# Low-rank parameter tiles in the places of the attention values, not in the residual stream's pool

## The chip, the cores and the metric

One NeuronCore of a Trainium2 chip runs the kernel. The metric is the device time of one execution in microseconds (us). The engines are named as in the profile: PE (TensorE, matmuls), PEld (its weight loads), DVE (VectorE), ACT (ScalarE), POOL (GpSimd) and SP (SyncE, which here only issues transfers).

## The reference

One layer of a streaming encoder, 512 tokens of width 1024, all in float32: a half-step SwiGLU, a mixer of two branches, a second half-step SwiGLU, and a final RMSNorm.

```python
x = x + 0.5 * swiglu(rms_norm(x, ffn1_norm[l]), ffn1_w1[l], ffn1_w3[l], ffn1_w2[l])
h = rms_norm(x, mix_norm[l])
p = h @ w_in[l]
p_rwkv = token_shift(p[..., :SHIFT_COLS], shift_mu[l])
p_fox = p[..., SHIFT_COLS:SHIFT_COLS + FOX_COLS]
gates = jax.nn.sigmoid(p[..., SHIFT_COLS + FOX_COLS:])
...
y_a = rwkv7_mixer(p_rwkv, ...) @ rwkv_proj[l]
y_b = fox_mixer(p_fox, f_bias, q_norm, k_norm) @ fox_proj[l]
x = x + (gate_a * y_a + gate_b * y_b) @ w_out[l]
x = x + 0.5 * swiglu(rms_norm(x, ffn2_norm[l]), ffn2_w1[l], ffn2_w3[l], ffn2_w2[l])
return rms_norm(x, final_norm)
```

What the change touches is the start of `rwkv7_mixer`. The decay and the in-context rate of its recurrence come from low-rank codes of the input projection, each through a small matrix of 32 rows:

```python
w_log = -jax.nn.softplus(-(w0 + jnp.tanh(w_lo) @ w_up)) - 0.5
a = jax.nn.sigmoid(a0 + a_lo @ a_up)
```

## The kernel before

Features lie on the 128 partitions and the 512 tokens along a row, so the residual stream is eight tiles `xT0` to `xT7` of 128 x 512. For accuracy each operand of a large matmul is split into a rounded part and the rest (`xh` and `xl`, `whi` and `wlo`), and a product is three matmuls (`mm3`, L130 to L132). A column of 128 outputs from 1024 inputs is therefore 24 matmuls. Its weights come as one transfer of 512 KB from SP's queue into `raw` (three buffers); ACT rounds them to `whi` (L122) and DVE takes the difference to `wlo` (L123), two buffers each. Columns of the projection go into a PSUM pool of two banks (`pm`), in turn.

The mixer begins at about 373 us with the low-rank codes (`pl`). Then come, for each of the four head pairs p, the columns k, r, v (`column`, PSUM `pk`) and a gate column (`plain_gate`, PSUM `pgt`), in the function `step(p)`. `column` empties the bank on DVE into a tile `u` (three buffers), multiplied by the norm's `rstd`, and `shifted` mixes `u` with its copy one token earlier, half on ACT, half on DVE. The key then gets its gain and its square (`ksq`, split into `khi` and `klo`), the sum of squares by a matmul `pn`, its inverse root (`krn`); the products go into `G` and `BK`, and `gp` are small matmuls between these.

Between the codes and the columns stand eight matmuls `pz` (L493): for each p one of `uw` (the matrix of the decay) and one of `ux` (that of the rate) with the codes. ACT turns each into a sigmoid (L494), DVE scans the decays along each chunk of 32 tokens with `cmask` (L565).

`uw` and `ux` are made early, on POOL, from `loraw`, which a transfer fills; `rows` holds the small parameters until one transpose puts them into `par`. The gains of the first norm come through a tile `g1` of their own.

Memory at the right edge is a stack of pools. The pool `xr1` holds the residual tiles `xT` and, before the change, also `g1`, `rows`, `loraw`, `uw` and `ux`. After the last `pz` is written down in the program, `xctx.close()` ends it (L496). Then `vtp` is opened, with four places `vt0` to `vt3` of 128 x 512 for the attention values (filled much later, at the columns `pv`) and a small pad, and above it `t2`, which holds `cmask`, `u`, the `k`/`r` tiles and the work tiles of `step`. A tile of a pool that takes over ended pools' memory waits until the ended pool's readers and writers are through. The residual itself has been saved by eight transfers `xsave` from POOL's queue (L408) and is read back later.

The order on each engine is set by a scheduler that simulates the program while it is built, from these waits, the order of the code and a few pins (`issue_after`, `keep_in_program_order`). A wait that vanishes can therefore change the order too.

Of the kernel before, what the change touches and what calls it, by code (L numbers as in the profile page):

```python
# [9 lines left out]
F32 = mybir.dt.float32  # L10
F32R = mybir.dt.float32r
# [7 lines left out]
P = 128  # L19
T = 512  # L20
# [4 lines left out]
DA = 512  # L25
# [3 lines left out]
NB = T // P  # L29
# [8 lines left out]
PAR_N = 69  # L38
# [13 lines left out]
def kernel(  # L52
# [6 lines left out]
    nc = tc.nc  # L59
    dve, act, pool, pe = nc.vector, nc.scalar, nc.gpsimd, nc.tensor  # L60
# [10 lines left out]
    def bank(name, pool_=None):  # L71
        pool_ = pool_ or pm
        return pool_.tile([P, T], F32, tag="b", name=name)
# [5 lines left out]
    ident = cp.tile([P, P], F32, name="ident")  # L79
# [76 lines left out]
        return cast  # L156


    xctx = ExitStack()
    rtp = xctx.enter_context(tc.tile_pool(name="xr1", bufs=1, side="right"))  # L160
    xT = [rtp.tile([P, T], F32, name=f"xT{c}") for c in range(KD)]
# [67 lines left out]
        return par[:, i:i + 1]  # L229


    g1 = rtp.tile([8, P], F32, name="g1")
    nc.scalar.dma_start(g1[:], ffn1_norm[0].rearrange("(a b) -> a b", b=P))
    warm = bank("warm", pf)
    for _ in range(8):
        pe.matmul(warm[:, 0:P], ones_[:], ones_[:], start=True, stop=True)
    gtp = bank("gtp", pr)
    pe.transpose(gtp[:, 0:8], g1[:], ident[0:8, 0:8])
    dve.tensor_copy(par[:, 0:8], gtp[:, 0:8])
    nrm = Norm(PAR_FFN1)  # L240
    with tc.tile_pool(name="x0", bufs=1) as x0:
# [26 lines left out]

    pin = pool.memset(onec[:], 1.0)
    tc.keep_in_program_order(pin)  # L270
    rows = rtp.tile([PAR_N, P], F32, name="rows")
    loraw = rtp.tile([P, DA], F32, name="loraw")
    uw, ux = [rtp.tile([96, DA], F32R, name=n) for n in ("uw", "ux")]
    q0, q1, q2 = slice(0, 32), slice(32, 64), slice(64, 96)

    def f32(ap):
        return ap.bitcast(F32)

    pool.memset(rows[:], 0.0)

    def masks():
        pool.memset(gmask[:], 1.0)
# [34 lines left out]

    def place_params():
        ptp = bank("ptp")
        pe.transpose(ptp[:, 0:PAR_N], rows[:], ident[0:PAR_N, 0:PAR_N])  # L320
        dve.tensor_copy(par[:, 8:PAR_N], ptp[:, 8:PAR_N])
        dve.tensor_scalar(par[:, PAR_Q:PAR_Q + 1], par[:, PAR_Q:PAR_Q + 1], 0.125, None, op0=ALU.mult)
        pool.tensor_copy(uw[q0], loraw[q0, :])
        pool.tensor_copy(uw[q1], loraw[q0, :])
        pool.tensor_tensor(uw[q2], loraw[q0, :], f32(uw[q0]), op=ALU.subtract)
        pool.tensor_copy(ux[q0], loraw[q1, :])
        pool.tensor_copy(ux[q2], loraw[q1, :])
        pool.tensor_copy(ux[q1], loraw[q1, :])
        pool.tensor_tensor(ux[q1], loraw[q1, :], f32(ux[q1]), op=ALU.subtract)
# [89 lines left out]
    with ExitStack() as mx:  # L419
# [74 lines left out]
                tc.keep_in_program_order(act.activation(o, ps[:], AF.Sigmoid, bias=pc(par0 + p)))  # L494
        logs = tc.keep_in_program_order(act.preload_act_table_set("natural_log_exp_and_others"))
        xctx.close()  # L496
        fctx = ExitStack()
        vtp = fctx.enter_context(tc.tile_pool(name="vtp", bufs=1, side="right"))
        vts = [vtp.tile([P, T], F32, name=f"vt{b}", tag=f"vt{b}") for b in range(NB)]
        vtp.tile([P, 48], F32, name="vtpad", tag="vtpad")  # L500
        pctx = ExitStack()
        t2 = pctx.enter_context(tc.tile_pool(name="t2", bufs=1, side="right"))
        cmask = t2.tile([P, T], F32, name="cmask")
# [148 lines left out]
        for t in range(C - 1):  # L652
            n, m = t + 1, C - 1 - t
# [67 lines left out]
        vt = []  # L721
# [109 lines left out]
        for p in range(NP):  # L831
# [16 lines left out]
            for i, bl in enumerate(((0, 1), (2,), (3,))):  # L848
# [3 lines left out]
                for q in range(2):  # L852
                    lp = pf.tile([P, T], F32, tag="b", name="lp")
                    lps.append(lp)
                    for b in bl:
                        n, bs = (b + 1) * P, slice(b * P, (b + 1) * P)
# [4 lines left out]
                for q in range(2):  # L861
                    pt, mx = pts[:, q], mx_[q]
                    for b in bl:
                        n, mb = (b + 1) * P, mx[:, b:b + 1]
# [107 lines left out]
        rtp = ctx.enter_context(tc.tile_pool(name="xr2", bufs=1, side="right"))  # L972
# [94 lines left out]
```

## Time and profile before

| | us |
|---|---|
| median of 3 runs | 1195.16 |
| lowest and highest | 1194.19, 1195.84 |
| the profiled execution's own time | 1195.16 |
| its span, first to last instruction | 1193.5 |

The mean granted clock of TensorE over the span is 0.994 of full speed. In the timeline a row begins with start and duration in us from the span's start; then come engine, line, operation, output and inputs, shapes, and in brackets how long the engine had been idle before it and what released it. Rows of waits give the total, the number of times and the longest. Rows of stretches give each engine's busy time with the number of instructions, then the granted clock, the share of the DMA engines and GB/s. Matmuls overlap, so their pace is read from start to start.

### The profile page before, as it was taken

The numbers are of one execution on the slowest core, as the hardware profiler recorded it, in microseconds if no ns is written. First come the engines' busy times: TensorE is split into PE (matmuls) and PEld (weight loads), VectorE is DVE, ScalarE is ACT, GpSimd is POOL, SyncE is SP. The second block draws the span as 40 slices with busy tenths as digits, with TensorE's granted clock in tenths as the row PEclk, the third lists the DMA queues.
The fourth block names the chain that finished last, engine by engine and source line by source line (L and its number), as shares of the span: only waits on it lengthen the run. The fifth ranks groups of instructions, "written<-read, shape, count | busy, mean of one in ns | idle before, by whom it ended". The sixth has DMA issues, their size and how long they took to land.

```text
span 1193.5 us, 15868 instructions
## 1 busy us (share of the span) xinstructions
PE 1172.4 (98%) x6334; PEld 953.9 (80%) x6334; DVE 663.8 (56%) x993; ACT 458.3 (38%) x739; POOL 101.1 (8%) x144
## 2 busy tenths in 40 slices
PE   8999999999999999999999999999999999999997
PEld 7888888888887788887767777778888888888887
DVE  6545444533444698676756657866554545443242
ACT  6322222222224755346876656523222222222221
POOL 4100000001111112301000011111000000000110
PEclk9999999999999999999999999999999999999999
DMA  7333333323333333344113135533333333323331
GB/s 199 89 105 90 95 100 97 97 87 115 114 113 107 96 102 117 103 137 115 54 37 95 54 99 173 186 107 93 102 89 106 89 106 88 105 81 97 97 97 71
DMA packets 208152, 122.54 MB, mean 103 GB/s; under 512 B 9902, under 2 KB 200430, under 8 KB 208078
## 3 DMA queue, kind: packets, MB, share of 16 engines
q1 hardware_dynamic: 202078, 108.67, 31.1%
q0 software_dynamic: 3760, 12.06, 3.1%
q8 instruction: 50, 0.82, 0.3%
q10 hardware_dynamic: 2240, 0.79, 0.3%
q14 instruction: 24, 0.20, 0.0%
HBM read 110.82 MB, written 10.68 MB: 102 GB/s over the span
## 4 chain that ended last, share of the span: by engine, by line
PE 94%; DVE 3%; ACT 1%; DMA 1%; issue 0%; SPq 0%; POOL 0%; DVEq 0%; POOLq 0%
PE pd L131 7%; PE pd L130 7%; PE pd L132 7%; PE pa L132 7%; PE pa L130 7%; PE pb L132 7%; PE pb L130 7%; PE pa L131 7%; PE pb L131 7%; PE pgt L130 3%; PE pgt L132 2%; PE pgt L131 2%; PE pk L130 2%; PE pk L132 2%; PE pk L131 2%; PE pw L132 1%
## 5 line engine op out<-in xcount | busy, mean ns | idle before, releaser
L122 ACT CAST whi<-raw 128x1024 fp32r<-128x1024 f32 (+2 forms) x197 | 196.4, 998 | 605.8 <-PE pa L131 176.0
L123 DVE TENSOR_TENSOR wlo<-raw,whi 128x1024 fp32r<-128x1024 f32 (+2 forms) x197 | 227.6, 1155 | 131.9 <-ACT whi L122 131.9
L132 PE MATMUL pa<-xh,wlo 128*128 128x512 f32 x344 | 133.9, 389 | 0.0
L131 PE MATMUL pa<-xl,whi 128*128 128x512 f32 x344 | 133.8, 389 | 0.0
L130 PE MATMUL pa<-xh,whi 128*128 128x512 f32 x344 | 133.8, 389 | 0.0
L132 PE MATMUL pb<-xh,wlo 128*128 128x512 f32 x344 | 133.8, 389 | 0.0
L130 PE MATMUL pb<-xh,whi 128*128 128x512 f32 x344 | 133.8, 389 | 0.0
L131 PE MATMUL pb<-xl,whi 128*128 128x512 f32 x344 | 133.8, 389 | 0.0
L132 PE MATMUL pd<-hh,wlo 128*128 128x512 f32 x330 | 129.0, 391 | 0.0
L131 PE MATMUL pd<-hl,whi 128*128 128x512 f32 x330 | 128.5, 389 | 0.0
L130 PE MATMUL pd<-hh,whi 128*128 128x512 f32 x330 | 128.4, 389 | 0.0
L343 DVE TENSOR_TENSOR fb<-pb,rstd 128x512 f32<-128x512 f32 x43 | 29.7, 691 | 137.2 <-PE pb L132 137.2
L131 PEld LDWEIGHTS pa<-xl,whi 128*128 128x128 f32 x344 | 64.6, 188 | 13.5
L132 PEld LDWEIGHTS pb<-xh,wlo 128*128 128x128 f32 x344 | 64.6, 188 | 13.5
L132 PEld LDWEIGHTS pa<-xh,wlo 128*128 128x128 f32 x344 | 64.5, 188 | 13.5
L130 PEld LDWEIGHTS pb<-xh,whi 128*128 128x128 f32 x344 | 64.6, 188 | 13.4
L130 PEld LDWEIGHTS pa<-xh,whi 128*128 128x128 f32 x344 | 64.5, 188 | 13.4
L131 PEld LDWEIGHTS pb<-xl,whi 128*128 128x128 f32 x344 | 64.5, 188 | 13.4
L131 PEld LDWEIGHTS pd<-hl,whi 128*128 128x128 f32 x330 | 61.9, 188 | 12.9
L130 PEld LDWEIGHTS pd<-hh,whi 128*128 128x128 f32 x330 | 62.0, 188 | 12.7
L132 PEld LDWEIGHTS pd<-hh,wlo 128*128 128x128 f32 x330 | 62.0, 188 | 12.7
L339 DVE TENSOR_TENSOR fa<-pa,rstd 128x512 f32<-128x512 f32 x43 | 29.7, 692 | 68.5 <-PE pa L132 68.4
(397 smaller groups left out, 1971.8 us busy)
## 6 DMA issues: line engine op xcount, KB each, us to landing
raw<-in_ffn_w_dram SPq DMA_DIRECT2D x116, 512.0 KB
raw<-in_w_in_dram SPq DMA_DIRECT2D x40, 512.0 KB
raw<-in_ffn_w_dram SPq DMA_DIRECT2D x15, 384.0 KB
raw<-in_w_out_dram SPq DMA_DIRECT2D x8, 512.0 KB
gsave<-gs SPq DMA_DIRECT2D x9, 256.0 KB
xin<-in_x_dram SPq DMA_DIRECT2D x4, 512.0 KB
xsave<-xT POOLq DMA_DIRECT2D x8, 256.0 KB, 2.3
G<-gsave POOLq DMA_DIRECT2D x8, 256.0 KB, 3.8
```

Of the source, the lines that this page charges most:

```text
L122: act.copy(hi[:], raw[:])
L123: (eng or dve).tensor_tensor(lo[:], raw[:], hi[:].bitcast(F32), op=ALU.subtract)
L130: pe.matmul(ps, whi, xhi, start=first, stop=False)
L131: pe.matmul(ps, whi, xlo, start=False, stop=False)
L132: return pe.matmul(ps, wlo, xhi, start=False, stop=last)
L339: dve.tensor_tensor(a[:], pa[:], nrm.rstd[:], op=ALU.mult)
L343: dve.tensor_tensor(b[:], pb[:], nrm.rstd[:], op=ALU.mult)
```

## The change

The pool `vtp` is opened at the very beginning, beneath the residual's pool. A helper `place(b, name)` hands out a tile in place `vt{b}`. `uw` and `ux` lie in places 0 and 1, `g1` and after it `loraw` in place 2, `rows` in place 3. When the residual's pool ends, `vtp` stays open, and the attention values take the four places as before. Each place has one buffer, so a new tile in it waits for the readers of the one before. The computation is the same; lines move down by 4 to 7.

```diff
+    fctx = ExitStack()
+    vtp = fctx.enter_context(tc.tile_pool(name="vtp", bufs=1, side="right"))
+
+    def place(b, name, dt=F32):
+        return vtp.tile([P, T], dt, name=name, tag=f"vt{b}")
+
     xctx = ExitStack()
     rtp = xctx.enter_context(tc.tile_pool(name="xr1", bufs=1, side="right"))
     xT = [rtp.tile([P, T], F32, name=f"xT{c}") for c in range(KD)]
...
-    g1 = rtp.tile([8, P], F32, name="g1")
+    g1 = place(2, "g1")[0:8, 0:P]
...
-    rows = rtp.tile([PAR_N, P], F32, name="rows")
-    loraw = rtp.tile([P, DA], F32, name="loraw")
-    uw, ux = [rtp.tile([96, DA], F32R, name=n) for n in ("uw", "ux")]
+    rows = place(3, "rows")[0:PAR_N, 0:P]
+    loraw = place(2, "loraw")
+    uw, ux = place(0, "uw", F32R), place(1, "ux", F32R)
+    vtp.tile([P, 48], F32, name="vtpad", tag="vtpad")
...
         xctx.close()
-        fctx = ExitStack()
-        vtp = fctx.enter_context(tc.tile_pool(name="vtp", bufs=1, side="right"))
-        vts = [vtp.tile([P, T], F32, name=f"vt{b}", tag=f"vt{b}") for b in range(NB)]
-        vtp.tile([P, 48], F32, name="vtpad", tag="vtpad")
+        vts = [place(b, f"vt{b}") for b in range(NB)]
```

More of the change, by code (lines that the diff above doesn't have):

```diff
@@ L229, in pc @@
         return par[:, i:i + 1]
-    g1 = rtp.tile([8, P], F32, name="g1")
-    nc.scalar.dma_start(g1[:], ffn1_norm[0].rearrange("(a b) -> a b", b=P))
+    g1 = place(2, "g1")[0:8, 0:P]
+    nc.scalar.dma_start(g1, ffn1_norm[0].rearrange("(a b) -> a b", b=P))
     warm = bank("warm", pf)
@@ L237 @@
     gtp = bank("gtp", pr)
-    pe.transpose(gtp[:, 0:8], g1[:], ident[0:8, 0:8])
+    pe.transpose(gtp[:, 0:8], g1, ident[0:8, 0:8])
     dve.tensor_copy(par[:, 0:8], gtp[:, 0:8])
@@ L277, in f32 @@
         return ap.bitcast(F32)
-    pool.memset(rows[:], 0.0)
+    pool.memset(rows, 0.0)
     def masks():
@@ L319, in place_params @@
         ptp = bank("ptp")
-        pe.transpose(ptp[:, 0:PAR_N], rows[:], ident[0:PAR_N, 0:PAR_N])
+        pe.transpose(ptp[:, 0:PAR_N], rows, ident[0:PAR_N, 0:PAR_N])
         dve.tensor_copy(par[:, 8:PAR_N], ptp[:, 8:PAR_N])
```

## The prediction

> **What bounds the kernel now.** I read the page, then TensorE's waits around the start of the mixer, then the timeline of PE, ACT and DVE there, then the clock by stretches. The page first:
>
> ```profile
> span 1193.5 us, 15868 instructions
> PE 1172.4 (98%) x6334; PEld 953.9 (80%) x6334; DVE 663.8 (56%) x993; ACT 458.3 (38%) x739; POOL 101.1 (8%) x144
> PE 94%; DVE 3%; ACT 1%; DMA 1%; issue 0%; SPq 0%; POOL 0%; DVEq 0%; POOLq 0%
> ```
>
> PE is the bound: 94% of the chain that ended last. Only places where PE stands still or runs slowly can be won. TensorE's waits from 370 to 470 us are two, both where the low-rank products `pz` meet the first key column:
>
> ```profile
> PE pz L493 <- ACT G L494: 0.8, 1, 0.8
> PE pk L130 <- DVE u L529: 0.8, 1, 0.8
> ```
>
> PE's rows there (start, duration, line; starts are what to read, since durations overlap):
>
> ```profile
> 384.88 0.48 PE L130 MATMUL pk<-xh,whi 128*128 128x512 f32 x1
> ...
> 397.08 0.39 PE L132 MATMUL pk<-xh,wlo 128*128 128x512 f32 x1
> 398.26 0.50 PE L493 MATMUL pz<-codes,uw 96*128 96x512 f32 x1 [0.80 <-ACT G L494]
> 398.84 0.51 PE L493 MATMUL pz<-codes,ux 96*128 96x512 f32 x1
> 400.13 0.50 PE L130 MATMUL pk<-xh,whi 128*128 128x512 f32 x1 [0.78 <-DVE u L529]
> ...
> 400.93 0.63 PE L130 MATMUL pk<-xh,whi 128*128 128x512 f32 x1
> 401.36 0.63 PE L131 MATMUL pk<-xl,whi 128*128 128x512 f32 x1
> ...
> 404.34 0.39 PE L132 MATMUL pk<-xh,wlo 128*128 128x512 f32 x1
> ...
> 407.29 0.39 PE L130 MATMUL pgt<-xh,whi 128*128 128x512 f32 x1
> ```
>
> I number the columns (24 matmuls each) as they stand on PE: c1 = k, c2 = r, c3 = v, c4 = the gate `pgt`, c5 = the next k. 384.88 is c1's first matmul, 397.08 c2's last, 400.13 c3's first, 407.29 c4's first. c3 needs the bank of c1, which only `u` (L529) empties, and `u` starts after the last `pz`:
>
> ```profile
> 399.38 1.29 DVE L529 TENSOR_TENSOR u<-pk,rstd 128x512 f32<-128x512 f32 x2 [0.50 <-PE pz L493]
> 399.42 0.52 POOL L504 MEMSET cmask<- 128x512 f32 x1 [24.75 <-PE pz L493]
> ```
>
> Why should `u` wait for a matmul that it doesn't read? Both `u` and `cmask` lie in the pool that takes over the residual's pool, and `ux`, which `pz` reads, is in that pool. The answer for the tile `ux` lists its waiters:
>
> ```profile
>   POOL cmask L504: 24.7, 1
>   DVE u L529: 0.5, 1
> ```
>
> c1 was complete 24 matmuls after 384.88, near 390.4 (at 0.227 us each, below); its `u` ran 9 us later for want of room, not of data. The second loss is the clock, in stretches of 3.41 us (PE busy, PEld, DVE, ACT, POOL, granted clock):
>
> ```profile
> 397.52:400.93 3.41, 1.81 (x6) 1.04 (x6) 2.52 (x3) 3.41 (x7) 1.48 (x6) 1.00 0.26 68
> 400.93:404.34 3.41, 3.41 (x10) 2.63 (x8) 2.55 (x3) 3.38 (x6) 0.78 (x4) 0.50 0.30 91
> 612.56:615.97 3.41, 1.47 (x14) 0.90 (x14) 3.25 (x8) 2.29 (x6) 0.00 (x0) 1.00 0.00 0
> 615.97:619.38 3.41, 3.41 (x16) 2.25 (x12) 2.76 (x8) 1.60 (x5) 0.00 (x0) 0.50 0.00 0
> 755.92:759.33 3.41, 1.83 (x8) 1.06 (x8) 2.23 (x4) 2.95 (x6) 0.00 (x0) 1.00 0.87 328
> ```
>
> After the thin stretch at 398 PE got half its clock for 3.41 us; starts stand 0.43 apart (400.93, 401.36) where 0.23 is normal. The same happened at 616, not after 756.
>
> **The change part by part.** `uw`, `ux`, `loraw` and `rows` leave the residual's pool for the attention values' places. The pool that holds `cmask`, `u`, `kt` now waits for the readers of the residual tiles alone. The last of these outside DVE and ACT is the eighth `xsave`, issued at
>
> ```profile
> 374.11 0.56 POOL L408 DMA_DIRECT2D xsave<-xT  x1 [0.84 <-DVE omu L441]
> xsave<-xT POOLq DMA_DIRECT2D x1, 256.0 KB, 2.5
> ```
>
> so landed by about 377.2 (374.11 + 0.56 + 2.5), 13 us before `u` wants the place. The instructions are the same in number; the scheduler lets three engines move. DVE before, from the low-rank codes on:
>
> ```order
> L485 TENSOR_TENSOR codes<-la,codes 32x512
> L482 TENSOR_TENSOR codes<-la,codes 32x512
> L123 TENSOR_TENSOR wlo<-raw,whi 128x1024 x2
> L529 TENSOR_TENSOR u<-pk,rstd 128x512 x2
> L565 SCALAR_TENSOR_TENSOR G_2715<-cmask,G_2715 128x512
> ```
>
> DVE with the change:
>
> ```order
> L492 TENSOR_TENSOR codes<-la,codes 32x512
> L533 TENSOR_TENSOR u<-pk,rstd 128x512
> L489 TENSOR_TENSOR codes<-la,codes 32x512
> L123 TENSOR_TENSOR wlo<-raw,whi 128x1024
> L454 SCALAR_TENSOR_TENSOR spare_2728<-u,par,spare_2728 128x511
> L155 TENSOR_TENSOR klo<-ksq,khi 128x512
> L533 TENSOR_TENSOR u<-pk,rstd 128x512
> ```
>
> c1's `u` now stands between the two splits of the codes, before c3's and c4's weight splits. ACT before, from the codes' casts on (`whi` is a column's rounded weights, first c3's, then c4's):
>
> ```order
> L480 CAST codes<-la 32x512
> L481 CAST codes<-la 32x512
> L122 CAST whi<-raw 128x1024 x2
> L494 ACTIVATE G_2715<-pz,par 128x512 x2
> L494 ACTIVATE G_2716<-pz,par 128x512 x2
> L494 ACTIVATE BK_2720<-pz,par 128x512 x2
> ```
>
> ACT with the change, from c3's cast on:
>
> ```order
> L122 CAST whi<-raw 128x1024
> L453 ACTIVATE spare_2728<-u,omu 128x512
> L561 ACTIVATE Tall<-spare_2728,par 128x512
> L563 ACTIVATE ksq<-Tall 128x512
> L154 CAST khi<-ksq 128x512
> L122 CAST whi<-raw 128x1024
> L501 ACTIVATE G_2719<-pz,par 128x512 x2
> ```
>
> Four operations of the key path (shift, key gain, square, its rounding) move ahead of c4's cast. On PE, the seventh and eighth `pz` move from before c3 to inside c4, behind 24 `pk` and one `pgt`; the small `gp` matmuls of the first head pair come some columns earlier, in the same 8 groups, so I charge them nothing.
>
> *The gain.* From 397.08 to 407.29 PE starts 27 matmuls (1 + 2 `pz` + 24) in 10.21 us. The normal step is that of the last 13 of c3: (407.29 - 404.34) / 13 = 0.227 us. 27 x 0.227 = 6.13, so 4.08 us are lost. Of these the half clock takes 3.41 - 8 x 0.227 = 1.59 (8 matmuls start from 400.93 up to 404.34), the waits 2.49. Both go if c3 follows c2 directly, since the `pz` then stand in a full stream.
>
> *What hides the moved work.* These rows bear it:
>
> ```profile
> 391.49 0.68 DVE L482 TENSOR_TENSOR codes<-la,codes 32x512 fp32r<-32x512 f32 x1 [1.13 <-ACT codes L480]
> 393.21 1.23 DVE L123 TENSOR_TENSOR wlo<-raw,whi 128x1024 fp32r<-128x1024 f32 x1 [1.04 <-ACT whi L122]
> 397.66 1.23 DVE L123 TENSOR_TENSOR wlo<-raw,whi 128x1024 fp32r<-128x1024 f32 x1 [3.22 <-ACT whi L122]
> 396.58 1.05 ACT L122 CAST whi<-raw 128x1024 fp32r<-128x1024 f32 x1 [3.40 <-PE pk L131]
> 397.53 2.41 ACT L494 ACTIVATE G<-pz,par 128x512 f32<-128x512 f32 x4
> 399.82 1.28 ACT L494 ACTIVATE BK<-pz,par 128x512 f32<-128x512 f32 x2
> 401.79 2.34 DVE L565 TENSOR_TENSOR_SCAN G<-cmask,G 128x512 f32<-128x512 f32 x2 [1.12 <-POOL cmask L505]
> 403.57 1.34 ACT L446 ACTIVATE spare<-u,omu 128x512 f32<-128x512 f32 x2
> 407.04 0.72 ACT L557 ACTIVATE Tall<-spare,par 128x512 f32<-128x512 f32 x1
> 411.06 0.81 ACT L563 ACTIVATE kt<-G,nka,par 128x512 f32<-128x512 f32 x1
> ```
>
> ACT idled 3.40 us before c4's cast, held by PE's c2. The four moved ones take about 0.67 + 0.72 and two more of that kind, at most 2.8 together: they fit, and the cast stays at 396.58. On DVE `u` (half of 1.29) fits the 1.13 before 391.49; the shift (0.7) and `klo` (0.7) fit the 3.22; the second `u`, which needs c2's end, puts c4's split from 397.66 to about 398.3, done by 399.5. c4 starts at 397.31 + 24 x 0.227 = 402.8: 3.3 us to spare. Without that cover each microsecond beyond it would stop PE for one.
>
> Next is c5. c4 with its two `pz` and two `pn` lasts 28 x 0.227, so c5 starts at 409.1. Its cast needs c3's end (402.5); ACT is then through six `pz` (401.1), one shift and `kt` (about 0.7 and 0.8): cast until about 403.6. DVE after 399.5: three scans (3 x 1.17) until 403.0, shift, `u` and the key product (3 x 0.7) until 405.1, split until 406.3: 2.8 us to spare. By the same count c6's split ends 2 to 3 us early, and the first `gp` finds its operands over 3 us early. From there DVE and ACT fall back into the old order about 4 us earlier, the inversion and the recurrence with them. On POOL `cmask` comes some 20 us sooner and the column of zeros goes ahead of the `RD` memsets, which now wait for the eighth `pz`; the `PC` copies and a gate's `gsave` stand behind them, and POOL has 8% to do. SP's order is unchanged; the load of `loraw` now also waits for the transpose of the first gains, near the start, and its result is needed by `pz` alone, hundreds of us later. I price these at 0; the bound is 1 us either way.
>
> *Sum.* The profiled execution took 1195.16, 1.66 around its span of 1193.5, and is the median of the three runs. 1195.16 - 4.08 = 1191.1.
>
> **A rule against the trace.** The Trainium skill, "TensorE: Matmul & The Clock Gate", Part 1, says that the half rate follows an idle window of about 3.4 us in a grid that runs free of the program. The trace agrees: 615.97 - 400.93 is 63 steps of 3.413. Its advice (§ Why this matters for your kernels) is to avoid idle gaps over about 3 us; here half clock came with PE busy 1.81 of 3.41 and no gap that long. By that advice there would be no half clock to win and the sum would be 1192.7; by the rows it is 1191.1, and the rows decide. By that rule the second half-speed stretch may come or go in any run, which is the first two rivals.
>
> **The rivals.** Threshold: 0.2% (2.4 us, 1192.8) is about what a measurement of this kernel tells from no change.
>
> 1. *The stretch after 616 goes too.* Its thin place shifts by 4.08 us, not a multiple of 3.41, so the grid may cut it in two. For it: the place at 756, as thin as that at 398, went unpunished. Against: a run's grid decides. Price: about 1.6 more, 1189.5.
> 2. *The half clock comes elsewhere,* as after 756, or stays somewhere near c3. Then only the waits are won: 1195.16 - 2.49 = 1192.7. For it: the three runs spread 1.65, one such stretch.
> 3. *The wait only moves.* If `u` still waits for the old pool, or c3 for its split, c3 starts when it did: 1195.2. Against it are the `xsave` rows and c3's split, done by 394.5.
> 4. *Slower: c4's cast comes late behind the key path.* ACT stands in order: if `u` or the squares were held, `whi` and all eight `pz` would be held with them. c4's margin is 3.3 us and the gain 4.1; each stop of PE brings a half clock of 1.6. Decisive from about 5.8 us of delay (3.3 + 4.1 - 1.6); at 8.5 it gives 1195.2 + 2.7 = 1197.9. Against it: the 3.40 us that ACT idled there.
>
> **How the numbers follow.** Forecast 1191.1: 0.55 (own range 1190.3 to 1192.0, from the 1 us on what I priced at 0). Rival 1: 0.17; 2: 0.12; 3: 0.11; 4: 0.05. Range 1189.2 to 1193.0 leaves out rivals 3 and 4, 0.16. Faster: 0.55 + 0.17 + half of rival 2, which lies on the threshold, 0.78; same 0.17; slower 0.05.
>
> **What would show it.** `u` near 390.6 on DVE; no PE wait in c3 or c4; full clock from 398 to 405; c4's first matmul near 402.8 and c5's near 409; everything behind about 4.1 earlier. A `u` that waits until the last `pz`, or a split that PE waits for in c4 to c8, would make it wrong.

## The result, and the profile after

The changed kernel takes 1190.76 us (median of 6 runs, 1189.53 to 1191.03). The kernel before, with three more runs beside it, takes 1194.68 (1191.77 to 1195.84). The ratio is 0.9967, 95% interval 0.9955 to 0.9978: faster by about 3.9 us. The prediction was 1191.1. One run of the kernel before in a later set, 1457.81 us at a mean granted clock of 0.751, is left out of the ratios and of the count of 64 runs below.

The page of the changed kernel, span and engines:

```profile
span 1188.5 us, 15870 instructions
PE 1169.2 (98%) x6334; PEld 952.3 (80%) x6334; DVE 662.1 (56%) x993; ACT 457.1 (38%) x739; POOL 100.4 (8%) x144
```

Its own time is 1190.24. PE has the same 6334 matmuls. `u` and `cmask` are gone from the list of the tile `ux`; one waiter is left (who waited, us in total, times):

```profile
  POOL RD L750: 26.5, 1
```

This one doesn't wait for `ux` itself: `RD`, a tile used later, takes the place of `codes`, which the same `pz` reads. The 26.5 us fall on POOL, which has time. What still holds the new pool is the last transfer `xsave`, and `cmask` is through long before 390:

```profile
377.41 0.52 POOL L508 MEMSET cmask<- 128x512 f32 x1 [2.07 <-DMA xsave<-xT]
```

PE waits for nothing from 370 to 470. Its rows from c1's first matmul to c5's first:

```profile
385.55 0.48 PE L130 MATMUL pk<-xh,whi 128*128 128x512 f32 x1
...
397.74 0.39 PE L132 MATMUL pk<-xh,wlo 128*128 128x512 f32 x1
397.97 0.39 PE L130 MATMUL pk<-xh,whi 128*128 128x512 f32 x1
...
403.41 0.39 PE L130 MATMUL pgt<-xh,whi 128*128 128x512 f32 x1
403.63 0.40 PE L500 MATMUL pz<-codes,uw 96*128 96x512 f32 x1
...
409.85 0.39 PE L130 MATMUL pk<-xh,whi 128*128 128x512 f32 x1
```

Everything stands 0.67 later from the start on (c1 at 385.55 against 384.88). c2's last matmul is at 397.74 and c3's first is 0.23 behind it. From there to c4's first pass 5.67 us for 25 matmuls, the normal step of 0.227. The clock there is full (the stretches that were thin and slow before):

```profile
397.52:400.93 3.41, 3.41 (x17) 2.82 (x16) 3.06 (x4) 3.41 (x6) 0.00 (x0) 1.00 0.26 78
400.93:404.34 3.41, 3.41 (x16) 2.81 (x15) 3.41 (x5) 3.41 (x6) 0.00 (x0) 1.00 0.58 154
608.61:612.02 3.41, 1.88 (x11) 1.20 (x9) 3.25 (x7) 2.35 (x6) 0.00 (x0) 1.00 0.00 0
612.02:615.43 3.41, 3.00 (x26) 2.12 (x28) 3.32 (x10) 2.67 (x8) 0.00 (x0) 1.00 0.00 0
```

The last two rows are the second thin place, that of 612.56 before: in this execution it brought no half clock. These two stretches don't lie on this execution's own grid of 3.413 us, which its half-speed stretch from 10.45 to 13.86 gives. On that grid the place is cut in two, 607.78 to 611.20 with PE busy 2.24 us and 611.20 to 614.61 with 2.64. DVE and ACT carry the moved work:

```profile
391.33 0.69 DVE L533 TENSOR_TENSOR u<-pk,rstd 128x512 f32<-128x512 f32 x1 [0.29 <-PE pk L132]
395.02 0.74 DVE L454 SCALAR_TENSOR_TENSOR spare<-u,par,spare 128x511 f32<-128x511 f32 x1
397.87 0.69 DVE L155 TENSOR_TENSOR klo<-ksq,khi 128x512 fp32r<-128x512 f32 x1 [2.10 <-ACT khi L154]
399.08 1.22 DVE L123 TENSOR_TENSOR wlo<-raw,whi 128x1024 fp32r<-128x1024 f32 x1
405.42 1.22 DVE L123 TENSOR_TENSOR wlo<-raw,whi 128x1024 fp32r<-128x1024 f32 x1
395.80 0.72 ACT L561 ACTIVATE Tall<-spare,par 128x512 f32<-128x512 f32 x1 [1.33 <-DVE spare L454]
397.75 1.05 ACT L122 CAST whi<-raw 128x1024 fp32r<-128x1024 f32 x1
```

`u` waits for PE's c1 and nothing else. c4's split is done at 400.3 for a start at 403.41, c5's at 406.64 for 409.85.

The span is 5.0 us shorter. The last step of DVE's triangular inversion shows what had been won before 612, in the kernel before and in the changed one:

```profile
542.31 0.22 DVE L657 TENSOR_TENSOR TT<-TT,prod 128x31 f32<-128x31 f32 x1
```

```profile
538.98 0.22 DVE L661 TENSOR_TENSOR TT<-TT,prod 128x31 f32<-128x31 f32 x1
```

That is 3.33 us: the 4.08 of the sum less the 0.67 of the later start leaves 3.41. The other 1.6 or so is the half-speed stretch at 616, which was not there this time.

### The profile page after: what moved, and what is told of

Read it like the earlier page. It is cut to its first block, busy times and chain, and to the rows that moved or that the text cites. A ratio compares the mean times of both kernels' runs of the same rounds, so it can differ in the third digit from the quotient of the medians.

```text
span 1188.5 us, 15870 instructions
## 1 busy us (share of the span) xinstructions
PE 1169.2 (98%) x6334; PEld 952.3 (80%) x6334; DVE 662.1 (56%) x993; ACT 457.1 (38%) x739; POOL 100.4 (8%) x144
## 4 chain that ended last, share of the span: by engine, by line
PE 95%; DVE 3%; ACT 1%; DMA 1%; issue 0%; POOL 0%; SPq 0%; DVEq 0%; POOLq 0%
PE pd L131 7%; PE pd L130 7%; PE pd L132 7%; PE pa L132 7%; PE pa L131 7%; PE pb L131 7%; PE pb L132 7%; PE pa L130 7%; PE pb L130 7%; PE pgt L130 3%; PE pgt L132 2%; PE pgt L131 2%; PE pk L130 2%; PE pk L132 2%; PE pk L131 2%; PE pw L132 1%
```

## The experiments

Theory A is that of the prediction: `u` waited for the ended pool's readers, and `pz`, which reads `uw` and `ux`, is the last of them. B says that the other tiles that moved count too, C that the early `cmask` brings the gain, D that the scheduler's new order of the key path on ACT does. Times are medians beside runs of the kernel before on the same chip.

**Which tiles.** Only `uw` and `ux` moved:

```diff
-    g1 = place(2, "g1")[0:8, 0:P]
+    g1 = rtp.tile([8, P], F32, name="g1")[:]
-    rows = place(3, "rows")[0:PAR_N, 0:P]
-    loraw = place(2, "loraw")
+    rows = rtp.tile([PAR_N, P], F32, name="rows")[:]
+    loraw = rtp.tile([P, DA], F32, name="loraw")
```

> The changed kernel, but g1, rows and loraw stay in the residual's pool; only uw and ux lie in the places. Theory A (room: u of the first key column waits only because uw and ux, which pz reads, lie in the ended pool): the wait is gone, c3 follows c2 directly, time as the changed kernel, 1189.5 to 1191.3 us. Theory B (all four tiles have to leave the pool): some wait of u on the pool stays, 1192.5 to 1195.

Measured: 1191.20 (1189.29 to 1192.88, 12 runs) beside 1194.86; ratio 0.9971, interval 0.9960 to 0.9981. As A said: the whole gain. `cmask` stood at 377 us and PE had no wait from 370 to 470.

The reverse, `uw` and `ux` back in the residual's pool, the rest moved:

```diff
-    uw, ux = place(0, "uw", F32R), place(1, "ux", F32R)
+    uw, ux = [rtp.tile([96, DA], F32R, name=n) for n in ("uw", "ux")]
```

> The changed kernel, but uw and ux stay in the residual's pool; g1, rows and loraw lie in the places. Theory A: nothing won, u starts after the last pz as before, the kernel's time as before, 1191.8 to 1195.8 us with a median near 1194.7, and half clock behind the gap in some runs. Theory B: part of the gain, 1191 to 1193.5.

Measured: 1194.89 (1192.93 to 1196.74, 12 runs), ratio 1.0005 (0.9995 to 1.0015). Nothing won. Its PE rows also separate the two losses, since this execution had the wait and not the half clock behind it:

```profile
396.69 0.40 PE L132 MATMUL pk<-xh,wlo 128*128 128x512 f32 x1
399.74 0.50 PE L130 MATMUL pk<-xh,whi 128*128 128x512 f32 x1 [0.78 <-DVE u L533]
...
405.30 0.39 PE L130 MATMUL pgt<-xh,whi 128*128 128x512 f32 x1
```

405.30 - 396.69 = 8.61 for the same 27 matmuls (6.13 at the normal step): the wait alone costs 2.48.

`ux` alone back:

```diff
-    uw, ux = place(0, "uw", F32R), place(1, "ux", F32R)
+    uw, ux = place(0, "uw", F32R), rtp.tile([96, DA], F32R, name="ux")
```

> The changed kernel, but ux alone goes back into the residual's pool; uw, g1, rows and loraw stay in the places. Theory A (one reader of the ended pool is enough to hold u): u starts only after the last pz, near 399, and PE idles before c3 as in the kernel before, 1192 to 1196 us. Theory B (each tile that leaves brings its share): u earlier than 398, time between the two kernels, near 1192.5.

Measured, one run: 1194.90, with the wait whole:

```profile
398.54 0.40 PE L132 MATMUL pk<-xh,wlo 128*128 128x512 f32 x1
400.84 1.29 DVE L533 TENSOR_TENSOR u<-pk,rstd 128x512 f32<-128x512 f32 x2 [0.50 <-PE pz L500]
407.17 0.39 PE L130 MATMUL pgt<-xh,whi 128*128 128x512 f32 x1
```

407.17 - 398.54 = 8.63. One tile left in the ended pool holds `u` as long as both do; B falls. The time of a single run says little, so this rests on the rows.

**Which waiter.** The kernel before, with `u` alone taken out of the pool:

```diff
-            u = t2.tile([P, T], F32, name="u", tag="u", bufs=3)
-            dve.tensor_tensor(u[:], ps[:], mix.rstd[:], op=ALU.mult)
+            u = Ls[:, turn[0] % 2]
+            turn[0] += 1
+            dve.tensor_tensor(u, ps[:], mix.rstd[:], op=ALU.mult)
```

> The kernel before, but u of the columns lies in two halves of Ls (free until the inversion) instead of the pool above the residual's; cmask, the squares and kt still wait for the last pz. Theory A (u alone holds PE): c3 follows c2, 1189.8 to 1191.8 us, though cmask still comes after the last pz. Theory C (the early cmask, whose memset waited 24.7 us, brings the gain through the scans): as before, about 1194.7.

Measured: 1191.31 (1189.16 to 1191.78, 9 runs), ratio 0.9971 (0.9960 to 0.9982). The whole gain, while `cmask` and the scans come even later than before (404.72 against 399.42, 407.09 against 401.79):

```profile
404.72 0.52 POOL L504 MEMSET cmask<- 128x512 f32 x1 [29.02 <-PE pz L493]
407.09 2.34 DVE L568 TENSOR_TENSOR_SCAN G<-cmask,G 128x512 f32<-128x512 f32 x2 [1.03 <-POOL cmask L505]
```

And `cmask` alone taken out:

```diff
-        cmask = t2.tile([P, T], F32, name="cmask")
+        cmask = Ls[:, 0]
```

> The kernel before, but cmask alone lies in Ls, so it is written early; u still waits for the last pz. Theory A: as before, median about 1194.7 us (1193.5 to 1195.8), PE idle before c3 as before. Theory C: the gain, about 1190.8.

Measured: 1194.49 (1192.59 to 1197.70, 12 runs), ratio 1.0002 (0.9992 to 1.0012). The mask is written at 372.79, and PE waits longer than before, since a scan slips ahead of `u`:

```profile
PE pk L130 <- DVE u L529: 1.3, 1, 1.3
372.79 0.53 POOL L504 MEMSET Ls<- 128x512 f32 x1 [11.49 <-PE pd L132]
399.58 1.26 DVE L529 TENSOR_TENSOR u<-pk,rstd 128x512 f32<-128x512 f32 x2
```

C falls: the longest wait in the list, 24.7 us, was worth nothing, and the one of 0.5 was worth the whole gain.

**Wait or order.** The changed kernel with the ACT half of the key's shift behind the `pz` activations again:

```diff
-            act.activation(o[0:rows, :], src[0:rows, :], AF.Copy, scale=omu[0:rows, mu - PAR_MU:mu - PAR_MU + 1])
+            with tc.issue_after(logs.ins) if mu == PAR_MU + 4 else ExitStack():
+                act.activation(o[0:rows, :], src[0:rows, :], AF.Copy, scale=omu[0:rows, mu - PAR_MU:mu - PAR_MU + 1])
```

> The changed kernel, but the ACT half of the key's shift is queued behind the table load after the eight pz activations, as ACT's order was before; the wait of u is gone all the same. Theory A (the wait, not the order, was worth the time): u near 391, c3 directly behind c2, 1189.5 to 1191.5 us. Theory D (the scheduler's new order of the key path on ACT brings the gain): 1193 to 1195.

Measured: 1191.11 (1189.07 to 1191.67, 6 runs) beside 1194.09, ratio 0.9966 (0.9954 to 0.9978). The key's shift ran at 406.00 on ACT, `u` at 390.38 on DVE, and PE had no wait from 370 to 470. D falls: the early key path was not needed for the gain.

**The clock.** The kernel before with PE kept busy in the gap:

```diff
-                pe.matmul(ps[:], w_[0:96, p * P:(p + 1) * P], x_[0:96, :], start=True, stop=True)
+                for _ in range(5 if p == NP - 1 and i else 1):
+                    pe.matmul(ps[:], w_[0:96, p * P:(p + 1) * P], x_[0:96, :], start=True, stop=True)
```

> The kernel before, but the last pz matmul is repeated four times more (the same result each time), so the wait of u gets longer by about 0.9 us and PE is busy in it. Clock theory (half clock follows a stretch in which PE is mostly idle): no half clock between 398 and 405 in any run that is looked at; the 0.9 us more of PE work are set against up to 1.6 less of half clock, median 1194.0 to 1195.3, and the fastest runs are about 0.9 slower than the fastest of before. Rival (half clock belongs to the place or the wait, not to idle PE): half clock stays as often, 0.9 us slower in the median, near 1195.7.

Measured: 1193.54 (1192.43 to 1194.55, 11 runs) beside 1194.09 (1192.33 to 1197.21, 17 runs); ratio 0.9992 (0.9983 to 1.0001). Four matmuls more and a later `u`, and yet not slower. The median is under my range, by 0.5; the fastest run is 0.10 above the fastest of before beside it, not the 0.9 that I expected, and why is open. In the profile the wait is 0.92 longer, as meant (3.97 us from c2's last matmul to c3's first, against 3.05), and c3 starts at full pace:

```profile
399.98 1.43 PE L494 MATMUL pz<-codes,ux 96*128 96x512 f32 x5
402.19 0.50 PE L130 MATMUL pk<-xh,whi 128*128 128x512 f32 x1 [0.78 <-DVE u L530]
402.53 0.40 PE L131 MATMUL pk<-xl,whi 128*128 128x512 f32 x1
402.76 0.40 PE L132 MATMUL pk<-xh,wlo 128*128 128x512 f32 x1
```

This profile alone doesn't decide, since the two executions above with the wait and no filling had full pace there too. Why is seen when the stretches are laid on each execution's own grid, stepped in 3.413 us from its half-speed stretches (PE busy of 3.41 us, then the clock in the stretch behind):

| execution | stretch or stretches with the wait | PE busy | clock behind |
|---|---|---|---|
| before | 397.52 to 400.93 | 1.81 | 0.50 |
| `cmask` alone out | 396.57 to 399.98 | 1.55 | 0.50 |
| `uw` and `ux` back | 395.14 to 398.55, 398.55 to 401.96 | 2.54, 2.63 | 1.00 |
| `ux` back | 397.08 to 400.49, 400.49 to 403.90 | 2.54, 2.63 | 1.00 |
| the gap filled | 395.89 to 399.30, 399.30 to 402.71 | 2.71, 2.45 | 1.00 |

Much the same wait brought half clock where the grid left it in one stretch, and none where the grid cut it in two. So it belongs to idle PE within one stretch, not to the wait as such; the rival falls by these rows. For the filling itself the runs' clocks speak: all 11 have a mean clock of 0.996 or 0.997, while of the 17 of before beside them 8 have 0.994 or less. That no unprofiled run with the filling had half clock there is read from these means only.

**A better version.** In the changed kernel the longest wait of PE in the merge, the columns `ppj` where the two branches come together, is for a weight cast:

```profile
PE ppj L130 <- ACT whi L122: 1.6, 1, 1.6
```

On ACT a table load (1.28 us) and three tanh of the gates stand ahead of that cast. Two of them, with the load, were queued behind the last exponential of the group norm, where ACT had 2.34 us idle:

```diff
-                act.activation(rn, rn, AF.Exp, scale=-0.5)
+                rooted = act.activation(rn, rn, AF.Exp, scale=-0.5)
-            late_tanh(m, parted)
+            late_tanh(m, rooted if m < 2 else parted)
```

> The changed kernel, and in addition the table load and the first two gate tanh of the merge stand behind the last exponential of the group norm instead of behind the last cast of the recurrence's output. In the changed kernel PE waits 1.6 us there for a weight cast that stands behind the load and three tanh on ACT. If that wait is ACT's queue: about 1.3 us less, 1189.5 us, with the wait at most 0.3. If the operands of those columns come late anyway (the bank, the output's cast): no change, 1190.9.

Measured: 1189.26 (1188.55 to 1190.49, 6 runs), ratio to before 0.9955 (0.9942 to 0.9968). The wait for the cast is gone; 0.4 stays, for a bank that a gate's DVE step empties:

```profile
746.49 1.28 ACT L972 ACT_TABLE_LOAD   x1
750.75 1.14 ACT L122 CAST whi<-raw 128x512 fp32r<-128x512 f32 x2 [0.78 <-PE ppj L131]
PE ppj L130 <- DVE ga L987: 0.4, 1, 0.4
```

That is a little over the 0.3 I had set. To compare the two on one chip:

> The changed kernel once more, beside the next one on the same chip. Median 1190.8 us (1189 to 1191.8); against the kernel before 3.3 to 4.2 less.

> The changed kernel with the two tanh and the table load behind the last exponential, once more. If the wait of 1.6 us for the weight cast was what they cost, its median lies 1.2 to 2.0 us under that of the changed kernel of the same set: 1.2 from the wait (0.4 of the 1.6 stays, for the gate's bank), and up to 0.4 from half clock after 755 that now comes less often. If the lower median of the run before was the chip's or the clock's chance: less than 0.6 apart.

Measured: 1190.74 (1189.61 to 1193.08, 10 runs) and 1189.40 (1187.57 to 1190.54, 7 runs), beside 1194.21; ratios 0.9971 (0.9959 to 0.9983) and 0.9962 (0.9949 to 0.9975). The medians differ by 1.34, within the range expected from the wait. The times and the intervals overlap, so the step is likely rather than shown; in the set before, the changed kernel itself did not run on the same chip.

## Why the prediction was right

- *The place and its cause.* `u` waited for room. The edits show it from both sides: `u` alone out of the new pool wins all, `uw` and `ux` alone out of the ended pool win all, and the rest wins nothing.
- *The sum, 4.08.* It is confirmed in the trace by 3.33 + 0.67 = 4.00 at the inversion's end. Of its two terms the waits, 2.49, measured 2.48 and 2.50 in two executions without half clock there. The half clock, 1.59, is real in the executions that have it (10.21 - 8.61 = 1.60), but not all have it: of the four kept executions with the wait unfilled, two. The sum was right for the stage. The two profiled executions differ by more, 4.92, since the stretch at 616 went too (1.6) and the start came 0.67 later. That the median came out 0.3 under the forecast is partly luck: 1195.16 was the median of three runs, 1194.68 that of six, and in the later set the medians stand 3.5 apart.
- *What hid the moved work.* c4's and c5's splits came 3.1 and 3.2 us ahead of need; I had said 3.3 and 2.8. One step was wrong: I put the four moved ACT operations into an idle time of 3.40 and left out that the key gain waits for DVE's half of the shift, which stands behind c3's split. ACT waited 1.33 for it, and c4's cast began at 397.75, 0.5 later than 396.58 + 0.67. The margin covered it.
- *Rival 1* came true in the profiled execution, by the cut that it named: on its own grid the place at 608 to 614 lies in two stretches (2.24 and 2.64 busy). It is not the rule: another execution of the changed kernel, whose grid has the place in one stretch (607.81 to 611.22, 1.47 busy), has half clock behind it:

```profile
610.00:615.00 5.00, 4.24 (x22) 2.84 (x21) 4.17 (x11) 2.42 (x7) 0.00 (x0) 0.66 0.00 0
```

- *Rival 2*, half clock elsewhere, is seen too: the kernel with only `uw` and `ux` moved, which has the gain at c3, had a half-speed stretch from 753 on:

```profile
750.00:755.00 5.00, 3.42 (x11) 2.12 (x10) 3.49 (x7) 4.15 (x7) 0.00 (x0) 0.83 0.79 290
755.00:760.00 5.00, 5.00 (x20) 4.06 (x19) 2.92 (x6) 2.40 (x5) 0.00 (x0) 0.83 0.35 103
```

  It took 1191.43 and not 1192.7: the stretch at 616, which rival 2 let stand, was gone in it.

- *Rivals 3 and 4* did not come: no wait took the place of the old one.

## What to carry to other kernels

When an instruction waits for something that it neither reads nor overwrites, ask whose memory its output lies in. A short-lived tile with a late reader, put into a pool that ends, can hold the first writers of the next pool (here `u` and `cmask`); give it a place whose next use is late. And rank waits by what stands behind them on the bounding engine: here 24.7 us on POOL cost nothing, and 0.5 on DVE cost 2.5 us, or 4.1 where half clock followed; the waits that PE shows there add up to 1.6.

## What the runs showed of the hardware

Half clock is a matter of each run as well as of the program: the program has the thin places, and each run's grid decides which of them lie in one stretch of 3.413 us. The Trainium skill, "TensorE: Matmul & The Clock Gate", Part 1, explains this by an activity window that runs free of the program; the runs agree, since the same thin places are slow in one execution and not in another.

How thin is too thin the twelve kept profiles bound, each on its own grid, start and end of the execution left out. Half clock followed stretches with PE busy 1.47 (twice), 1.55, 1.57, 1.64, 1.81 and 1.83 (three times) of 3.41 us. It did not follow 1.83 (once, at 755.92 before), 1.84, 1.85 (four times), 1.86, or any stretch with 2.03 and more. So in these kernels the limit lies near 1.83 us, a little over half, as this profile models a busy PE. No single wait of PE in the stretches at 398 and 612 was over 1.2 us; several short ones did it together.

The mean granted clock of a run tells of this only roughly. In the 64 runs of the kernel before that the experiments were compared with, 20 at 0.997 or more have a median of 1192.59, 18 at 0.995 or 0.996 one of 1195.0, 26 at 0.994 or less one of 1195.24. Of 16 runs of the changed kernel none is at 0.994 or less; 7 at 0.997 have a median of 1190.32, the other 9 one of 1191.03. Between the groups at 0.997 the gain is thus 2.3 us, near the 2.49 of the waits, and between the middle groups 4.0. But the mean also counts half clock at the start and the end of an execution: the later profile of the changed kernel reads 0.997 with a stretch at 611 and none at its start. And one run with `uw` and `ux` back reads 0.944 at an ordinary 1195.83.
